# Two pair blocks at the end of each expert stage, held on the chip, in a diffusion backbone on one Trainium2 core

## The chip, the core and the metric

The kernel runs as one program on one core of a Trainium2 chip. A core has a matrix engine (TensorE, PE in the profile; PEld is its loading of weights), a vector engine (VectorE, DVE), an engine for activations (ScalarE, ACT), a general engine (GpSimd, POOL), an engine that mostly issues DMAs (SyncE, SP), and 16 DMA engines. TensorE's results go to PSUM banks; everything else lives in on-chip SBUF. The metric is the time of one execution in microseconds on the device; the kernel before took 2634.41 us, the median of three runs (2627.93 to 2635.23).

## What is computed

Two layers over 512 latent tokens (and 256 context tokens in the first), each a token mixer and then a hierarchical mixture of experts: every token is sent to 2 of 32 experts, and the two results, weighted, are added to the token's row. The part that matters here:

```python
    out = lax.map(expert_block, (buf.reshape(n_blocks, MOE_BLOCK, d), block_expert)).reshape(cap, d)
    # expert_block: (silu(xb @ w_gate[e]) * (xb @ w_up[e])) @ w_down[e]
    y = jnp.zeros((n_assign, d), h.dtype).at[order].set(out[dest]).reshape(n_tok, TOP_K, d)
    return jnp.einsum('tk,tkd->td', weights, y)
...
        x = x + gt2 * hier_moe(...)       # d = 1024, hidden width 512, 32 experts, top 2
    return rmsnorm(x, final_g)
```

## The kernel before, in words

Class `Moe` (from line 324) does one expert stage; `m[0]` is layer 0 with n = 6 tiles of 128 tokens, `m[1]` layer 1 with n = 4. After routing, the 32 experts are ranked by their number of tokens. The `big` first ranks (8 in layer 0, 6 in layer 1) get a block of 128 rows each; the others share a block by twos, 64 rows each. So a stage has 20 units (12 pairs and 8 big ones) or 19 (13 and 6). `self.seq` (line 337) is their order: the pair of two experts that are fixed beforehand first, then big ones and pairs mixed evenly; in both layers it ends on a big one and a pair.

A unit's weights come in pieces of 1 MB (`load`, line 486): 6 for a big one, 12 for a pair, in the order gate, up, down. They go through a ring of slots (`slot`, line 451; 13 slots in layer 0, 15 in layer 1), all issued by SyncE in order (line 497). The unit's token rows are gathered from `hbuf` by GpSimd (line 811).

`experts` (line 842) is the loop over units: gate and up products into `gu_ps` (line 901), `hidden` (silu and product, lines 964 and 965), `transposed` (line 855: TensorE transposes into banks of tag `eT`, three of them, then a copy by ScalarE for `hT` or an add by VectorE for `xT`), the down products into `o_ps` (line 918), and `yo` (line 921: VectorE scales by the token's weight and the gate). `scatter` (line 824) writes yo's rows to `ybuf` in DRAM, two rows for each token (GpSimd, indirect DMA).

The last unit is not scattered. Its yo is split into two fp32r parts (`y_parts`, lines 66 and 67) and brought to token order by a product with a matrix of zeros and ones (`one_hot`, line 950), line 942. All other results come back from `ybuf` by `early` (line 869): one load for each tile of 128 tokens (line 874), 1 MB, into slots of the weight ring, issued behind the scatter of the next-to-last unit; GpSimd then adds the two rows of each token (line 877). The end of the stage (lines 933 to 947) goes tile by tile: for two tiles of three VectorE adds the reloaded row sum to x (line 937), for the third TensorE adds it by a product with the identity (line 944); VectorE adds the product to x (line 945); then `after.tile` takes the sum of squares (line 2113) and `after.group` the reciprocal root for a group of tiles (lines 78 to 90). In layer 0 (`Rms`) x goes to DRAM and the RWKV layer follows; in layer 1 (`FinalNorm`) line 2144 makes the results and line 2145 stores them. `overflow` (line 968) is a loop for blocks over 128 rows, which runs zero times if there are none; all engines pass its test.

The order of instructions on each engine is made by the framework's scheduler from the order of the program and its own model, except in `route`, where it is as written. `behind` and `late_table` (lines 737 and 792) are small tables for the overflow, made beside the units 6 and 7, and also use banks of tag `eT`.

Of the kernel before, what the change touches and what calls it, by code (L numbers as in the profile page):

```python
# [9 lines left out]
F32 = mybir.dt.float32  # L10
# [7 lines left out]
P = 128  # L18
# [305 lines left out]
class Moe:  # L324


    def __init__(self, k, l, n):
        self.k, self.l, self.n = k, l, n


        self.big = BIGS[l]
        self.pairs = (NE - self.big) // 2
        self.units = self.big + self.pairs

        self.nb = self.units + (2 * n * P) // 65
        rest, small = range(self.big), range(self.big, self.units - 1)
        self.seq = [self.units - 1] + [u for _, u in sorted(
            [((i + 0.5) / len(rest), u) for i, u in enumerate(rest)] + [((i + 0.6) / len(small), u) for i, u in enumerate(small)])]
        self.raw, self.slots = {}, 0
        self.scattered = []  # L340

# [13 lines left out]
    def open(self, ps, tag):  # L355
# [13 lines left out]
        self.tok = new([n], "tok")  # L369
# [146 lines left out]
    def route(self, rp, ps, after):  # L516
# [165 lines left out]
        u = self.seq[-1]  # L682
# [109 lines left out]
    def late_table(self, ep, ps, place, blocks, a, b, part):  # L792

        k, n, m = self.k, self.n, part.stop - part.start

        def hot(i, t):
            v = ep.tile([P, P], F32R, name="hot", bufs=2)
            k.nc.vector.tensor_scalar(v, k.iota, place[:, i, t:t + 1], None, op0=ALU.is_equal)
            return v

        def rows(i, shape):
            v = ep.tile([P, 512], F32R, name="h_e", bufs=2)[:, 0:n * m * (b - a)]
            return v.rearrange("p (n v b) -> p n v b", n=n, v=m)

        q = ps.tile([P, 4, b - a], F32, name="tab", tag="eT", bufs=3)
        self.table(k.nc.vector, q, rows, hot, blocks, a, b, part)

    def gather(self, b, idx=None):
# [33 lines left out]
    def experts(self, ep, ps, after):  # L842
# [12 lines left out]
        def transposed(src, nj, name, bufs, pin=False):  # L855
            T = ep.tile([P, nj, P], F32, name=name, bufs=bufs)
            for hf in range(nj // 4):
                q = ps.tile([P, 4, P], F32, name="eT_ps", tag="eT", bufs=3)
                for j in range(4):
                    turn = nc.tensor.transpose(q[:, j, :], self.block(src, 4 * hf + j) if nj == KD else src[:, j * P:(j + 1) * P], k.ident)  # L860
                    if pin and j + hf == 0:
                        k.tc.keep_in_program_order(turn)
                if nj == KD:
                    self.shifted(T, q, hf)
                else:
                    nc.scalar.copy(T, q)  # L866
            return T

        def early():

            ys = []
            for t in range(n):
                y = self.slot().rearrange("p (k d) -> p k d", k=2)
                nc.sync.dma_start(y, self.ybuf[2 * t * P:2 * (t + 1) * P, :].rearrange("(p k) d -> p k d", k=2))
                ys.append(y)
# [9 lines left out]
        for i in range(N + 1):  # L885
# [5 lines left out]
            if i < N:  # L891
                want(i + 1)
                if i + XG - 1 < N:
                    xg[i + XG - 1] = self.gather(seq[i + XG - 1])
                q = {}
                for gu in range(2):
                    q[gu] = ps.tile([P, 512], F32, name="gu_ps", tag="gu", bufs=2)
                    for kk in range(KD):
                        f = slice(kk % 4 * 512, kk % 4 * 512 + 512)
                        for r, rows in self.ranks(seq[i]):  # L900
                            mm(q[gu][rows], xT[i][:, kk, rows], self.raw[r, 2 * gu + kk // 4][:, f], start=kk == 0, stop=kk == KD - 1)  # L901
                    if i + gu == 0:
                        xT[1] = transposed(xg[1], KD, "xT", 2, True)
                h = self.hidden(ep, q)
            if i + 2 < N:
                xT[i + 2] = transposed(xg[i + 2], KD, "xT", 2)
            if i == N - 2:
                one_hot = self.one_hot(ep)
            if i >= 1:
                u = seq[i - 1]  # L910
                g = self.gate(ep, self.ctx[:, u:u + 1])
                yo = ep.tile([P, D], F32, name="yo", bufs=YO)
                o = [ps.tile([P, 512], F32, name="o_ps", tag="eo", bufs=2) for _ in range(2)]
                for c in range(4):
                    for hf in range(2):
                        f = slice(c % 2 * 1024 + hf * 512, c % 2 * 1024 + hf * 512 + 512)
                        for r, rows in self.ranks(u):
                            mm(o[hf][rows], hT[i - 1][:, c, rows], self.raw[r, 4 + c // 2][:, f], start=c == 0, stop=c == 3)  # L918
                for hf in range(2):
                    f = slice(hf * 512, hf * 512 + 512)  # L920
                    stt(yo[:, f], o[hf], self.wslot[:, u:u + 1], g[:, f], op0=ALU.mult, op1=ALU.mult)  # L921
                if i < N:
                    self.scatter(u, yo)
                    if i == N - 1:
                        ys = early()
                else:
                    yh, yl = (ep.tile([P, D], F32R, name="y_parts", tag="xT", bufs=2) for _ in range(2))
                    for hf in range(2):
                        f = slice(hf * 512, hf * 512 + 512)
                        split(k, yh[:, f], yl[:, f], yo[:, f])  # L930
            if i < N:
                hT[i] = transposed(h, 4, "hT", 2)
        for g in after.groups:
            for t in g:
                by_pe = t % 3 == 2
                if not by_pe:
                    k.tc.keep_in_program_order(tt(k.x[:, t, :], k.x[:, t, :], ys[t][:, 0, :], op=ALU.add))
                for hf in range(2):
                    f = slice(hf * 512, hf * 512 + 512)
                    q = ps.tile([P, 512], F32, name="c_ps", tag=("gu", "eo")[t % 2], bufs=2)  # L940
                    for j, y in enumerate((yh, yl)):
                        mm(q, one_hot[:, t * P:(t + 1) * P], y[:, f], start=(j == 0), stop=(j == 1 and not by_pe))
# [7 lines left out]
    def one_hot(self, ep):  # L950

        k = self.k
        oh = self.xgp.tile([P, D], F32R, name="xg", bufs=XG)
        for t in range(self.n):
            k.tc.keep_in_program_order(k.nc.vector.tensor_scalar(
                oh[:, t * P:(t + 1) * P], k.iota, self.tok[:, t:t + 1], None, op0=ALU.is_equal))
        return oh

    def hidden(self, ep, q):
# [8 lines left out]
    def overflow(self, ep, ps, after):  # L968
# [5 lines left out]
        with tc.For_i(0, nv) as i:  # L974
# [14 lines left out]
            xg = self.gather(None, idx)  # L989
            xT = self.xgp.tile([P, D], F32, name="xg", bufs=XG).rearrange("p (k s) -> p k s", k=KD)  # L990
            for hf in range(2):
                q = ps.tile([P, 4, P], F32, name="eT_ps", tag="eT", bufs=3)
# [13 lines left out]
            qh = ps.tile([P, 4, P], F32, name="eT_ps", tag="eT", bufs=3)  # L1006
# [32 lines left out]
BIGS, KNOWN = (8, 6), 2  # L1039

RAW = (2, 8, 3), (4, 6, 5)
XG, YO = 4, 3


C = 64
# [1053 lines left out]

class Rms:  # L2100

    groups = ((0, 1), (2, 3), (4, 5))

    def __init__(self, k):
        self.k = k
# [148 lines left out]
```

## Time and profile before

| | us |
|---|---|
| median of the runs (lowest, highest) | 2634.41 (2627.93, 2635.23) |
| the profiled execution | 2646.03 |
| its span, first to last instruction | 2644.2 |
| TensorE busy | 2374.9 (90%) |
| VectorE busy | 1096.4 (41%) |
| ScalarE busy | 723.5 (27%) |
| GpSimd busy | 374.3 (14%) |
| HBM read and written | 580.65 MB and 76.02 MB |

The profiled execution took 11.6 us more than the median. The profile divides its span in 40 equal slices of 66.1 us and gives the busy share of each engine in tenths, the clock that TensorE was granted (1.00 is 2.4 GHz, 0.50 is 1.2 GHz, means lie between), and the DMA engines' mean share and rate. In a timeline a row is one instruction or several alike in sequence (x4): start, time from the first's start to the last's end, engine, line, operation, what it writes and reads. A value in brackets is the engine's idle time just before, and what ended it. TensorE's fp32 products are recorded as two matmuls each, fp32r products as one.

### The profile page before, as it was taken

The numbers are of one execution on the slowest core, as the hardware profiler recorded it, in microseconds if no ns is written. First come the engines' busy times: TensorE is split into PE (matmuls) and PEld (weight loads), VectorE is DVE, ScalarE is ACT, GpSimd is POOL, SyncE is SP. The second block draws the span as 40 slices with busy tenths as digits, with TensorE's granted clock in tenths as the row PEclk, the third lists the DMA queues.
The fourth block names the chain that finished last, engine by engine and source line by source line (L and its number), as shares of the span: only waits on it lengthen the run. The fifth ranks groups of instructions, "written<-read, shape, count | busy, mean of one in ns | idle before, by whom it ended". The sixth has DMA issues, their size and how long they took to land. (4 is left out here: it accounts for less than half of the span.)

```text
span 2644.2 us, 38930 instructions
## 1 busy us (share of the span) xinstructions
PE 2374.9 (90%) x15546; PEld 1503.5 (57%) x15546; DVE 1096.4 (41%) x2016; ACT 723.5 (27%) x1225; POOL 374.3 (14%) x316
## 2 busy tenths in 40 slices
PE   5999999997999999968979899888888799999984
PEld 2878997774434334336745488777877543333331
DVE  3334333443122111178655364887787412211114
ACT  3222213331000000036644246556544200000001
POOL 0000000003332322230012112112212110000001
PEclk8999999997999999979978698989999899999997
DMA  7135316558999999943165464434335699999993
GB/s 249 57 128 187 116 65 212 198 214 345 398 421 393 421 413 421 398 149 100 57 192 160 139 180 122 102 89 98 85 94 167 234 418 420 421 416 413 420 416 158
DMA packets 280077, 640.24 MB, mean 242 GB/s; under 512 B 131084, under 2 KB 156940, under 8 KB 229460
## 3 DMA queue, kind: packets, MB, share of 16 engines
q1 hardware_dynamic: 266548, 608.69, 62.6%
q0 software_dynamic: 11904, 23.77, 2.4%
q10 hardware_dynamic: 1440, 5.24, 0.5%
q8 instruction: 124, 2.03, 0.3%
q14 instruction: 61, 0.50, 0.1%
HBM read 580.65 MB, written 76.02 MB: 248 GB/s over the span
## 5 line engine op out<-in xcount | busy, mean ns | idle before, releaser
L901 PE MATMUL gu_ps<-e_raw,xT 128*64 128x512 f32 (+1 forms) x2048 | 582.7, 596 | 15.7 <-DMA e_raw<-moe_w_up 13.5
L901 PEld LDWEIGHTS gu_ps<-e_raw,xT 128*64 128x64 f32 (+1 forms) x2048 | 210.0, 148 | 371.1 <-issue 324.0
L918 PE MATMUL o_ps<-e_raw,hT 128*64 128x512 f32 (+1 forms) x1024 | 295.9, 603 | 5.0 <-ACT hT L866 5.0
L965 DVE TENSOR_TENSOR h_e<-gu_ps,h_e 128x512 f32<-128x512 f32 x39 | 27.0, 692 | 483.2 <-PE gu_ps L901 483.2
L918 PEld LDWEIGHTS o_ps<-e_raw,hT 128*64 128x64 f32 (+1 forms) x1024 | 105.7, 149 | 157.2 <-issue 142.9
L964 ACT ACTIVATE h_e<-gu_ps 128x512 f32<-128x512 f32 x39 | 23.3, 597 | 568.3 <-PE gu_ps L901 568.3
L1134 PE MATMUL p<-ident 128*128 128x128 f32 x892 | 138.4, 298 | 8.8 <-ACT BKt L1819 4.7
L1134 PEld LDWEIGHTS p<-ident 128*128 128x128 f32 x892 | 116.6, 201 | 21.2 <-ACT BKt L1819 6.5
L866 ACT COPY hT<-eT_ps 128x512 f32<-128x512 f32 x39 | 22.9, 586 | 349.4 <-PE eT_ps L860 349.4
L825 POOL DMA_INDIRECT ybuf<-yo,idx x37 | 37.0, 1000 | 456.3 <-DVE yo L921 401.2
L921 DVE SCALAR_TENSOR_TENSOR yo<-o_ps,wslot,gt_e 128x512 f32<-128x512 f32 x40 | 30.0, 751 | 170.6 <-issue 120.7
L811 POOL DMA_INDIRECT xg<-hbuf,idx x39 | 41.4, 1061 | 397.3 <-PE eT_ps L860 322.3
L73 PE MATMUL u_ps<-hh,w_hi 128*128 128x384 f32 x256 | 90.2, 353 | 4.8 <-ACT w_hi L66 4.8
L921 DVE SCALAR_TENSOR_TENSOR yo<-o_ps,wslot,gt2B 128x512 f32<-128x512 f32 x38 | 28.5, 751 | 153.0 <-PE o_ps L918 151.3
L75 PE MATMUL u_ps<-hh,w_lo 128*128 128x384 f32 x256 | 86.0, 340 | 1.2 <-DVE w_lo L67 1.2
L74 PE MATMUL u_ps<-hl,w_hi 128*128 128x384 f32 x256 | 87.0, 340 | 0.0
L67 DVE TENSOR_TENSOR w_lo<-w_raw,w_hi 128x1024 fp32r<-128x1024 f32 x56 | 68.1, 1222 | 40.4 <-ACT w_hi L66 39.7
L123 PE MATMUL ada_ps<-w_raw,cstat 128*32 128x512 f32 x384 | 63.8, 633 | 20.6 <-DMA w_raw<-ada_w 20.3
L73 PE MATMUL v_ps<-w_hi,hh 128*128 128x512 f32 x192 | 75.5, 406 | 4.2 <-ACT w_hi L66 4.2
L1849 DVE TENSOR_TENSOR X<-X,subt 128x31 f32<-128x31 f32 (+15 forms) x186 | 75.2, 404 | 5.2 <-DVE subt L1844 0.2
L66 ACT CAST w_hi<-w_raw 128x1024 fp32r<-128x1024 f32 x56 | 58.5, 1048 | 64.4 <-DMA w_raw<-ga_w_out 28.4
L75 PE MATMUL v_ps<-w_hi,hl 128*128 128x512 f32 x192 | 75.7, 394 | 0.0
(561 smaller groups left out, 4444.9 us busy)
## 6 DMA issues: line engine op xcount, KB each, us to landing
e_raw<-moe_w_gate SPq DMA_DIRECT2D x128, 1024.0 KB
e_raw<-moe_w_up SPq DMA_DIRECT2D x128, 1024.0 KB
e_raw<-moe_w_down SPq DMA_DIRECT2D x128, 1024.0 KB
w_raw<-ada_w SPq DMA_DIRECT2D x96, 512.0 KB
w_raw<-ga_w_in SPq DMA_DIRECT2D x32, 512.0 KB
Td<-c_st SPq DMA_DIRECT2D x64, 192.0 KB
T<-Td SPq DMA_DIRECT2D x24, 512.0 KB
ybuf<-zero_rows SPq DMA_DIRECT2D x20, 512.0 KB
```

Source lines behind the costliest of these rows:

```text
L66: k.nc.scalar.copy(hi, src)
L67: k.nc.vector.tensor_tensor(lo, src, hi.bitcast(F32), op=ALU.subtract)
L73: mm(out, a[0], b[0], start=start, stop=False)
L74: mm(out, a[0], b[1], start=False, stop=False)
L75: mm(out, a[1], b[0], start=False, stop=stop)
L123: nc.tensor.matmul(q[32 * g:32 * g + 32, :], k.cstat[:, j, :], w, start=(j < 4), stop=(j >= 4), tile_position=(0, 32 * g))
L811: k.nc.gpsimd.indirect_dma_start(out=xg[:], out_offset=None, in_=self.hbuf[:, :], in_offset=bass.IndirectOffsetOnAxis(ap=self.idx[:, 1, b: ...
L901: mm(q[gu][rows], xT[i][:, kk, rows], self.raw[r, 2 * gu + kk // 4][:, f], start=kk == 0, stop=kk == KD - 1)
L918: mm(o[hf][rows], hT[i - 1][:, c, rows], self.raw[r, 4 + c // 2][:, f], start=c == 0, stop=c == 3)
L921: stt(yo[:, f], o[hf], self.wslot[:, u:u + 1], g[:, f], op0=ALU.mult, op1=ALU.mult)
L1134: nc.tensor.matmul(q[:, 0:128], self.ident, self.ident, start=True, stop=True)
L1849: eng.tensor_tensor(x, x, t.t.rearrange("p (a b) -> p a b", a=31 - j), op=ALU.subtract)
```

## The change

- `HELD = 2`: the last two units of `seq` are pairs, taken from the end of the ranks; the others are mixed as before. In layer 0 the order was P PBPBPBPPBPBPBPPBPBP and becomes P BPPBPBPBPBPBPBPBPPP; in layer 1 it was P PBPPBPPBPPBPPBPPBP and becomes P PBPBPPBPPBPBPPBPPP (P a pair, B a big one).
- Neither of the two is scattered. The down products of the next-to-last unit come ahead of the last unit's gate and up; its two parts take buffers of the ring `yo`, and its products into token order (`add`) are placed one step (tile and half) at a time between the last unit's gate and up products, in banks of tag `c` and `eT` alternately, each followed by VectorE's add to x.
- `early` is called ahead of that, behind the last weights. GpSimd adds no rows. At the end, for even tiles VectorE adds both reloaded rows to x; for odd tiles TensorE adds both by identity products in the bank of the last unit's rows.
- Tag `eT` has two banks in place of three, the third goes to `c`. `tok` is made by one broadcast add for each held unit. A square root of one column is put behind the last silu. Layer 0's groups become (0, 1, 2, 3) and (4, 5).

```diff
+        small, last = small[:len(small) - HELD], list(small[len(small) - HELD:])
         self.seq = [self.units - 1] + [u for _, u in sorted(
-            [((i + 0.5) / len(rest), u) ...] + [((i + 0.6) / len(small), u) for i, u in enumerate(small)])]
+            [((i + 0.5) / len(rest), u) ...] + [((i + 0.6) / len(small), u) for i, u in enumerate(small)])] + last
...
-        for t in range(n):
-            ts(self.tok[:, t:t + 1], tab[0][:, 1, u:u + 1], float(BIG - t * P), None, op0=ALU.add)
+        for i, u in enumerate(self.seq[-HELD:]):
+            tt(self.tok[:, i, :], tab[0][:, 1, u:u + 1].to_broadcast([P, n]), self.off, op=ALU.add)
...
-                q = ps.tile([P, 4, P], F32, name="eT_ps", tag="eT", bufs=3)
+                q = ps.tile([P, 4, P], F32, name="eT_ps", tag="eT", bufs=2)
...
             for t in range(n):
-                y = self.slot().rearrange("p (k d) -> p k d", k=2)
-                nc.sync.dma_start(y, self.ybuf[2 * t * P:2 * (t + 1) * P, :]...)
-            for y in ys:
-                nc.gpsimd.tensor_tensor(y[:, 0, :], y[:, 0, :], y[:, 1, :], op=ALU.add)
+                ys.append(self.slot().rearrange("p (k d) -> p k d", k=2))
+                nc.sync.dma_start(ys[t], self.ybuf[2 * t * P:2 * (t + 1) * P, :]...)
...
+        def output(i):
...
+            parts = None
+            if i >= N - HELD:
+                tag, bufs = ("yo", YO) if i < N - 1 else ("xT", 2)
+                parts = [ep.tile([P, D], F32R, name="y_parts", tag=tag, bufs=bufs) for _ in range(2)]
...
+            if not parts:
+                self.scatter(u, yo)
+            return parts
+
+        def add(one_hot, parts, t, hf, tag, more=()):
+            q = ps.tile([P, 512], F32, name="c_ps", tag=tag, bufs=2 if tag != "c" else 1)
+            for j, y in enumerate(parts):
+                mm(q, one_hot[:, t * P:(t + 1) * P], y[:, half(hf)], start=(j == 0), stop=(j == 1 and not more))
+            for j, y in enumerate(more):
+                mm(q, k.ident, y[:, half(hf)], start=False, stop=(j + 1 == len(more)))
+            tt(k.x[:, t, half(hf)], k.x[:, t, half(hf)], q, op=ALU.add)
...
+            if i == N - 1:
+                ys = early()
+                hot = self.one_hot(0)
+                parts = output(i - 1)
+                steps = [(t, hf) for t in range(n) for hf in range(2)]
...
+                    if steps and gu * KD + kk > 2:
+                        t, hf = steps.pop(0)
+                        add(hot, parts, t, hf, ("c", "eT")[hf])
...
+            if 1 <= i < N - 1:
+                output(i - 1)
+            if i == N - 1:
+                hot = self.one_hot(1)
+                nc.scalar.activation(self.sm.tile([P, 1], F32, name="root"), k.ones[:, 0:1], AF.Sqrt)
+            hT[i] = transposed(h, 4, "hT", 2)
+        parts = output(N - 1)
+        junk = self.xgp.tile([P, D], F32, name="xg", bufs=XG)
         for g in after.groups:
             for t in g:
-                by_pe = t % 3 == 2
-                if not by_pe:
-                    k.tc.keep_in_program_order(tt(k.x[:, t, :], k.x[:, t, :], ys[t][:, 0, :], op=ALU.add))
+                if t % 2 == 0:
+                    for y in range(2):
+                        tt(k.x[:, t, :], k.x[:, t, :], ys[t][:, y, :], op=ALU.add)
                 for hf in range(2):
...
-                    if by_pe:
-                        nc.tensor.matmul(q, k.ident, ys[t][:, 0, f], start=False, stop=True)
-                    tt(k.x[:, t, f], k.x[:, t, f], q, op=ALU.add)
-                after.tile(t, ys[t][:, 1, :])
+                    add(hot, parts, t, hf, ("gu", "eo")[t % 2], [ys[t][:, y, :] for y in range(2)] if t % 2 else ())
+                after.tile(t, junk)
...
-    groups = ((0, 1), (2, 3), (4, 5))
+    groups = ((0, 1, 2, 3), (4, 5))
```

## Rows read from the trace of the kernel before

**Rows 1.** The page: DMA share of 40 slices in tenths.

```profile
DMA  7135316558999999943165464434335699999993
```

**Rows 2.** Windows: busy time of each engine, granted clock, DMA share, GB/s.

```profile
core 0: us, PE busy (x) PEld busy (x) DVE busy (x) ACT busy (x) POOL busy (x), PEclk, DMA share, GB/s
...
760.00:780.00 20.00, 16.46 (x68) 6.82 (x64) 10.20 (x35) 0.59 (x1) 3.48 (x2) 0.83 1.01 419
...
2560.00:2580.00 20.00, 18.42 (x47) 7.37 (x45) 2.22 (x6) 1.18 (x2) 0.00 (x0) 1.00 1.01 419
...
2580.00:2590.00 10.00, 10.00 (x49) 3.43 (x50) 0.75 (x1) 0.60 (x1) 0.97 (x1) 1.00 0.62 257
...
2610.00:2620.00 10.00, 6.52 (x14) 3.35 (x12) 7.24 (x9) 3.78 (x6) 1.40 (x1) 0.59 0.00 0
```

**Rows 3.** Timeline of PE, two waits for weights: start, us, what, idle before.

```profile
650.85 3.65 PE L901 MATMUL gu_ps<-e_raw,xT 128*64 128x512 f32 x16 [1.68 <-DMA e_raw<-moe_w_up]
...
2541.93 3.65 PE L901 MATMUL gu_ps<-e_raw,xT 128*64 128x512 f32 x14 [1.30 <-DMA e_raw<-moe_w_up]
```

**Rows 4.** Timeline of SP: issues of weights and of the reload.

```profile
1094.92 7.75 SPq L497 DMA_DIRECT2D e_raw<-moe_w_down  x4
...
2512.80 9.07 SPq L497 DMA_DIRECT2D e_raw<-moe_w_up  x4
...
2569.94 7.77 SPq L497 DMA_DIRECT2D e_raw<-moe_w_down  x4
2589.37 1.86 SPq L874 DMA_DIRECT2D e_raw<-ybuf  x4
```

**Rows 5.** Timeline of PE: the last unit's down products in either layer.

```profile
1122.09 7.14 PE L918 MATMUL o_ps<-e_raw,hT 128*64 128x512 f32 x32 [0.73 <-ACT hT L866]
...
2596.15 7.14 PE L918 MATMUL o_ps<-e_raw,hT 128*64 128x512 f32 x32 [0.73 <-ACT hT L866]
```

**Rows 6.** Timeline of POOL: its adds of reloaded rows in either layer.

```profile
1126.26 16.84 POOL L877 TENSOR_TENSOR e_raw<-e_raw 128x1024 f32<-128x1024 f32 x6 [18.19 <-DMA e_raw<-ybuf]
...
2601.13 10.27 POOL L877 TENSOR_TENSOR e_raw<-e_raw 128x1024 f32<-128x1024 f32 x4 [19.06 <-DMA e_raw<-ybuf]
```

**Rows 7.** Timeline of DVE (last row ACT): layer 0's last operation, layer 1's end.

```profile
1160.87 0.16 DVE L90 TENSOR_TENSOR rstd<-r34s,r34t 128x2 f32<-128x2 f32 x1
...
2602.47 1.61 DVE L921 SCALAR_TENSOR_TENSOR yo<-o_ps,wslot,gt2B 128x512 f32<-128x512 f32 x2 [7.76 <-PE o_ps L918]
2604.00 5.19 DVE L67 TENSOR_TENSOR y_parts<-yo,y_parts 128x512 fp32r<-128x512 f32 x2
2609.11 3.37 DVE L937 TENSOR_TENSOR x_res<-x_res,e_raw 128x1024 f32<-128x1024 f32 x1
...
2613.79 1.22 DVE L937 TENSOR_TENSOR x_res<-x_res,e_raw 128x1024 f32<-128x1024 f32 x1
2615.04 1.28 DVE L945 TENSOR_TENSOR x_res<-x_res,c_ps 128x512 f32<-128x512 f32 x2
...
2631.57 1.28 DVE L2144 SCALAR_TENSOR_TENSOR yo<-x_res,rstd,fgB 128x1024 f32<-128x1024 f32 x1
...
2629.00 1.06 ACT L2113 ACTIVATE e_raw<-x_res 128x1024 f32<-128x1024 f32 x1 [4.83 <-DMA out_dram<-yo]
```

**Rows 8.** Timeline of PE: fp32r products, transposes, identity products, a big unit.

```profile
250.40 0.34 PE L73 MATMUL u_ps<-hh,w_hi 128*128 128x384 f32 x1
250.57 0.34 PE L74 MATMUL u_ps<-hl,w_hi 128*128 128x384 f32 x1
...
923.44 1.49 PE L860 MATMUL eT_ps<-ident,xg 128*128 128x128 f32 x8
...
1143.52 3.60 PE L944 MATMUL c_ps<-e_raw,ident 128*128 128x512 f32 x4
...
2555.46 14.00 PE L901 MATMUL gu_ps<-e_raw,xT 128*128 128x512 f32 x32
```

**Rows 9.** The instructions of line 684: ns shortest/median/longest.

```profile
L684 DVE TENSOR_SCALAR tok<-tab x10: 134/136/136, 611.2 to 2100.7; 128x1 f32<-128x1 f32 x10
```

More of the change, by code (lines that the diff above doesn't have):

```diff
@@ L336, in __init__ @@
         rest, small = range(self.big), range(self.big, self.units - 1)
+        small, last = small[:len(small) - HELD], list(small[len(small) - HELD:])
         self.seq = [self.units - 1] + [u for _, u in sorted(
-            [((i + 0.5) / len(rest), u) for i, u in enumerate(rest)] + [((i + 0.6) / len(small), u) for i, u in enumerate(small)])]
+            [((i + 0.5) / len(rest), u) for i, u in enumerate(rest)] + [((i + 0.6) / len(small), u) for i, u in enumerate(small)])] + last
         self.raw, self.slots = {}, 0
@@ L368, in open @@
         self.wslot, self.ctx = new([self.nb], "wslot"), new([self.nb], "ctx")
-        self.tok = new([n], "tok")
+        self.tok, self.off = new([HELD, n], "tok"), new([n], "tok_off")
+        ts(self.off, k.iota[:, 0:n], -float(P), float(BIG), op0=ALU.mult, op1=ALU.add)
         self.oh = new([2, n, 32], "oh")
@@ L803, in rows @@
             return v.rearrange("p (n v b) -> p n v b", n=n, v=m)
-        q = ps.tile([P, 4, b - a], F32, name="tab", tag="eT", bufs=3)
+        q = ps.tile([P, 4, b - a], F32, name="tab", tag="eT", bufs=2)
         self.table(k.nc.vector, q, rows, hot, blocks, a, b, part)
@@ L872, in early, with half @@
             for t in range(n):
-                y = self.slot().rearrange("p (k d) -> p k d", k=2)
-                nc.sync.dma_start(y, self.ybuf[2 * t * P:2 * (t + 1) * P, :].rearrange("(p k) d -> p k d", k=2))
-                ys.append(y)
-            for y in ys:
-                nc.gpsimd.tensor_tensor(y[:, 0, :], y[:, 0, :], y[:, 1, :], op=ALU.add)
-            return ys
+                ys.append(self.slot().rearrange("p (k d) -> p k d", k=2))
+                nc.sync.dma_start(ys[t], self.ybuf[2 * t * P:2 * (t + 1) * P, :].rearrange("(p k) d -> p k d", k=2))
+            return ys
+        def half(hf):
+            return slice(hf * 512, hf * 512 + 512)
+        def output(i):
+            u = seq[i]
+            g = self.gate(ep, self.ctx[:, u:u + 1])
+            yo = ep.tile([P, D], F32, name="yo", bufs=YO)
+            o = [ps.tile([P, 512], F32, name="o_ps", tag="eo", bufs=2) for _ in range(2)]
+            for c in range(4):
+                for hf in range(2):
+                    f = slice(c % 2 * 1024 + hf * 512, c % 2 * 1024 + hf * 512 + 512)
+                    for r, rows in self.ranks(u):
+                        mm(o[hf][rows], hT[i][:, c, rows], self.raw[r, 4 + c // 2][:, f], start=c == 0, stop=c == 3)
+            parts = None
+            if i >= N - HELD:
+                tag, bufs = ("yo", YO) if i < N - 1 else ("xT", 2)
+                parts = [ep.tile([P, D], F32R, name="y_parts", tag=tag, bufs=bufs) for _ in range(2)]
+            for hf in range(2):
+                stt(yo[:, half(hf)], o[hf], self.wslot[:, u:u + 1], g[:, half(hf)], op0=ALU.mult, op1=ALU.mult)
+                if parts:
+                    split(k, parts[0][:, half(hf)], parts[1][:, half(hf)], yo[:, half(hf)])
+            if not parts:
[8 more added lines that the diff above has]
+            tt(k.x[:, t, half(hf)], k.x[:, t, half(hf)], q, op=ALU.add)
         xg, xT, hT = {}, {}, {}
@@ L884, in experts @@
         xT[0] = transposed(xg[0], KD, "xT", 2)
-        for i in range(N + 1):
+        for i in range(N):
             if i == BEHIND:
@@ L890, in experts @@
                     self.late_table(ep, ps, self.place_ov, self.block_ov, self.units, self.nb, part)
[L891 to L904, printed above, removed]
+            want(i + 1)
@@ new lines, in experts @@
+            if i + XG - 1 < N:
+                xg[i + XG - 1] = self.gather(seq[i + XG - 1])
+            steps = []
+            if i == N - 1:
[3 more added lines that the diff above has]
+                steps = [(t, hf) for t in range(n) for hf in range(2)]
+            q = {}
+            for gu in range(2):
+                q[gu] = ps.tile([P, 512], F32, name="gu_ps", tag="gu", bufs=2)
+                for kk in range(KD):
+                    f = slice(kk % 4 * 512, kk % 4 * 512 + 512)
+                    for r, rows in self.ranks(seq[i]):
+                        mm(q[gu][rows], xT[i][:, kk, rows], self.raw[r, 2 * gu + kk // 4][:, f], start=kk == 0, stop=kk == KD - 1)
+                    if steps and gu * KD + kk > 2:
+                        t, hf = steps.pop(0)
+                        add(hot, parts, t, hf, ("c", "eT")[hf])
+                if i + gu == 0:
+                    xT[1] = transposed(xg[1], KD, "xT", 2, True)
@@ L905, in experts @@
+            h = self.hidden(ep, q)
             if i + 2 < N:
                 xT[i + 2] = transposed(xg[i + 2], KD, "xT", 2)
[L907 to L930, printed above, removed]
@@ L938, in experts @@
                 for hf in range(2):
[L939 to L942, printed above, removed]
-                    if by_pe:
-                        nc.tensor.matmul(q, k.ident, ys[t][:, 0, f], start=False, stop=True)
-                    tt(k.x[:, t, f], k.x[:, t, f], q, op=ALU.add)
@@ L955, in one_hot @@
             k.tc.keep_in_program_order(k.nc.vector.tensor_scalar(
[L956 removed]
+                oh[:, t * P:(t + 1) * P], k.iota, self.tok[:, i, t:t + 1], None, op0=ALU.is_equal))
         return oh
@@ L991, in overflow @@
             for hf in range(2):
-                q = ps.tile([P, 4, P], F32, name="eT_ps", tag="eT", bufs=3)
+                q = ps.tile([P, 4, P], F32, name="eT_ps", tag="eT", bufs=2)
                 for j in range(4):
@@ L1005, in overflow @@
             hT = ep.tile([P, 4, P], F32, name="hTo", tag="h_e", bufs=2)
-            qh = ps.tile([P, 4, P], F32, name="eT_ps", tag="eT", bufs=3)
+            qh = ps.tile([P, 4, P], F32, name="eT_ps", tag="eT", bufs=2)
             for j in range(4):
@@ L1041 @@
 RAW = (2, 8, 3), (4, 6, 5)
-XG, YO = 4, 3
+XG, YO, HELD = 4, 3, 2
 C = 64
```

5 lines of the change are left out of this document (1 added, 4 removed).

## The prediction

> **What bounds the kernel now.** I read the page's slices first: DMA engines are busy at 9 tenths in the 11th to 17th and the 33rd to 39th slice [rows 1]. Those are the two expert stages, layer 0 until some 1130 us and layer 1 from some 2110 to 2603. Only their ends, and what follows until the next stage, can be touched by this change, so the second view is the windows of the ends and the third the timelines there, engine by engine.
>
> In layer 1 weights arrive without a gap (419 GB/s, share 1.01) until 2580, then the share falls to 0.62 [rows 2]. TensorE is busy 18.4 of 20 us, yet it still waits for weights at 2541.93 [rows 3]. When does the last weight land? SyncE issued the piece awaited there as the last of four at 2512.80 + 9.07 - 0.33 = 2521.5; TensorE went on at 2541.93. So a piece lands 20.4 us after its issue. The last weight was issued at 2569.94 + 7.77 - 0.33 = 2577.4 [rows 4], so it lands near 2597.8, although the share falls at 2580: some DMA engines are done early while others still have a backlog. The last product uses it from its second half on, 2596.15 + 3.57 = 2599.7, and ends at 2603.29 [rows 5]. There TensorE has 1.9 us of slack against DMA. With the same lag layer 0's last weight lands at 1094.92 + 7.75 - 0.33 + 20.4 = 1122.7 against a use at 1122.09 + 3.57 = 1125.7: slack 3.0 us, end 1129.23.
>
> Behind that end stands a chain on VectorE. GpSimd adds the two rows of each token (10.27 us in layer 1, 16.84 in layer 0), because the reload of rows waited for a scatter: issued 2589.37, landed 2601.13 [rows 4, 6]. While GpSimd adds, VectorE's operations are stretched: two halves of y_parts take 5.19 us and the first row add 3.37; the same add later takes 1.22 [rows 7]. From the last product to the last result VectorE's chain is 2632.85 - 2603.29 = 29.6 us in layer 1 and 1161.03 - 1129.23 = 31.8 us in layer 0 [rows 5, 7].
>
> **The change part by part.**
>
> *Order of units, scatter gone.* The weights are the same 192 pieces per layer. One scatter, of the next-to-last unit, falls away: 0.5 MB, at 419 GB/s an estimate of 1.25 us of DMA time ahead of the last weight. Layer 1 ends on pair, pair, pair. Each pair brings 12 MB (30 us at that rate) and costs TensorE 14 us of gate and up, 7.1 of down, 2.2 of turns between, about 23. So at this end TensorE waits for DMA: last weight 2597.8 - 1.25 = 2596.6, then half a product, 3.57, gives 2600.2, with 0.2 for the wake-up 2600.4: **2.9 us earlier**. Layer 0 is different: there TensorE runs without waits (its only long one is 1.68 us at 650.85 [rows 3]), a ring of 13 pieces lets DMA lead by one pair only, and pair, pair, pair at the end uses up that lead without emptying it. So its end goes with TensorE's own work, bounded below by DMA: 1122.7 - 1.25 + 3.57 = 1125.0, that is -4.2 us.
>
> *Held products.* The next-to-last unit's rows are added by fp32r products inside the last unit's gate and up: 6 tiles x 2 halves x 2 parts = 24 in layer 0, 16 in layer 1. One of 384 columns follows the next after 0.17 us [rows 8]; for 512 I estimate 0.23. That is 5.5 us and 3.7 us. In layer 1 they lie in waits for weights: from 2571, when the unit before is done by the same lag, 14 + 3.7 us reach 2588.7, while the last up piece is used until 2590. In layer 0 nothing covers them: +5.5 on the path. VectorE's 12 (8) adds of 0.64 (two in 1.28 [rows 7]) run under them; each step waits for the bank that the add two steps before empties (0.46 + 0.64 us against 1.8 us for two steps), and behind a step that waits stand the last unit's gate and up on TensorE, so its whole end.
>
> *Transposes with two banks in place of three.* hT takes one bank, xT two; xT's second half must now wait for the copy of hT. Eight transposes take 1.49 us [rows 8], so the second half begins 0.75 us behind hT's last one, by when ScalarE has had as long for its copy of hT: next to nothing in steady state. During the late tables, which hold a bank, TensorE already idles 3.5 us in 20 [rows 2]; bounds 0 and +5 a layer (that idle time once more and half again); I take +0.5, nearest to the steady state, in layer 0 and none in layer 1, where a wait for weights follows. The first waits of layer 0 (unit 1 becomes a big one): -2.0 to 0, I take -2.0. So layer 0's last product ends at +5.5 - 2.0 + 0.5 = **+4.0** (bounds -4.2 to +10).
>
> *Reload.* It is issued behind the weights without the scatter's wait. On the engines that are late it follows the weights at once as before, so in layer 1 the four land from 2601.13 - 1.25 = 2599.9 on, 2.5 us apart; the chain wants them at about 2602.5, 2604, 2608 and 2608.5. It costs and wins nothing by itself. Between it and the weights nothing else stands on SyncE; behind it wait only the stores of x, which need the sums anyway. In layer 0 the six rows need 15 us behind the weights, up to 1137 or 1141, and are wanted from 1135 to 1150.
>
> *VectorE's chain, layer 1.* GpSimd's adds are gone, and with them the stretching. From the end of the product: 2.1 us until y_parts are done (two halves at 0.65, about half a row add each, the first 0.8 behind the product with its half of yo and a cast); tile 0 has two row adds of 1.22 and two product adds in 1.28: 5.8; tile 1 two product adds: 7.1; tile 2 with 0.5 for small operations: 11.3; five small operations of 0.2: 12.3; two results of 1.24: 14.8; six small ones 16.0; a result 17.3; tile 3: 18.6; square 1.06 and its read-out 0.2, small ones 1.4, the last result 1.28: 22.5 [rows 7]. TensorE must keep up: an odd tile now has four fp32r and four identity products, the latter two records each of 0.44 (32 such records in 14.00 us [rows 8]): 0.9 + 3.5 = 4.4 us at the high clock, an even one 0.9, so 5.3 us a couple of tiles against VectorE's 5.2. I add 1.5 us for waits: 24.0 against 29.6, **-5.6**.
> *Layer 0* in the same way: 2.1 + 3 x 5.2 + 1.0 (first group's small ones, one group fewer) + 1.3 + 2.9 (last square and its small ones) = 22.9, with 0.8 of wake-ups 23.7, and 2.5 for TensorE: 26.2 against 31.8, **-5.6**. What follows, the loop test and the next stage, shifts with it.
> *Routing:* ten operations of 0.136 [rows 9] become four of like size: -0.7 (bounds -0.8 to 0). The first operand "off", the second one-hot and the early square root lie beside other work: one sits in phase A's end, the others under products; without that cover each costs under 1.3 us.
>
> Sum: layer 0 +4.0 - 5.6 = -1.6; layer 1 -2.9 - 5.6 = -8.5; routing -0.7; together **-10.8**. The profiled execution took 2646.0 (span 2644.2), so it would take 2635.2; the median of the runs is 2634.4, 11.6 lower, and goes to **2623.6**, written 2624. 0.3% is 7.9 us, about what a measurement can tell from no change: below 2626.5 is faster, above 2642.3 slower.
>
> **The rivals.**
> 1. *DMA is really done when its share falls.* For it: 0.62 from 2580 [rows 2], 257 GB/s for 10 us or 2.6 MB, which would end the weights at some 2587. Then in layer 1 the product ends 2587 + 3.8 = 2591, 12 us earlier in place of 2.9, and the sum is -20: 2614. Against it: the lag of 20.4 us, and the first row's landing at 2601.13, 11.8 us behind its issue. The Trainium skill (DMA: Bandwidth & Descriptors, "Why a DMA increments its semaphore by 16 and not by 1") says that a transfer runs on up to 16 engines that finish independently and has landed only with the last of them. By that rule a mean share can't date the last weight and the forecast stands, by the share alone this rival would; no row here shows the engines apart. Chance 0.14.
> 2. *The end side is eaten in layer 0.* Two banks delay turns and late tables, held products wait for their one bank "c": the product ends at +10 in place of +4, and VectorE's order puts a row add in front of yo before its row has landed (+2.5). Sum -2.3: 2632. For it: layer 0 has no cover. Chance 0.24.
> 3. *TensorE at the low clock bounds both tails: slower.* The granted clock is 0.59 in the tail [rows 2], a mix of 2.4 and 1.2 GHz, after TensorE had stood with little work between its last product and y_parts. At 1.2 GHz four identity records take 3.60 us in layer 0's tail [rows 8], 0.88 each with pipelining; an odd tile takes 4 x 0.46 + 8 x 0.88 = 8.9 us, a couple 10.7. Layer 1's tail is then 2.5 + 2 x 10.7 + 4.8 = 28.7 (-0.9), layer 0's 2.5 + 3 x 10.7 + 3.7 = 38.3 (+6.5). Sum: 4.0 + 6.5 - 2.9 - 0.9 - 0.7 = +6.0: 2640, and 2646 with layer 0's product at +10. It is slower than before from 9.5 us a couple on (five couples, 6 us over 5 below 10.7). Against it: TensorE now has work almost all the time from y_parts on. Chance 0.14.
>
> **How the numbers follow.** Forecast 0.48, between -4 and -18 by the bounds; some 0.35 of it lies below 2626.5. With rival 1 faster has 0.49. Rival 3 has half beyond 2642.3, rival 2 and the forecast's tail 0.03 more: slower 0.10. Same: 0.41. The range goes from 2609 (rival 1 with the lower bound of layer 0's end) to 2640 (rival 3), which leaves out about 0.17.
>
> **What would show it.** Right: no GpSimd add; y_parts at 0.7 us a half; layer 1's last product ends 2 to 4 us earlier by the stage's own start, with waits for the last down piece; layer 0's ends up to 10 us later. Wrong: an end 10 us earlier in layer 1 (rival 1), VectorE waiting for c_ps of odd tiles several us each with clock near 0.5 (rival 3), TensorE gaps before transposes (rival 2), or VectorE waiting for a reload ahead of yo.

## The result, and the profile after

The changed kernel takes 2656.0 us (median of 10 runs, 2651.3 to 2664.7) beside 2640.2 (10 runs, 2627.9 to 2644.7) of the kernel before: ratio 1.0061, interval 1.0044 to 1.0078. It is **slower by 0.6%**, where 2624 was predicted and 2640 was the upper end of the range. The profiled execution took 2656.15 us (span 2654.4) beside 2646.03 (span 2644.2). Stage by stage, in us of the two profiled executions:

| stretch | before | after | change | predicted |
|---|---|---|---|---|
| layer 0, first gate product to end of last down product | 505.0 | 532.3 | +27.3 | +4.0 |
| layer 0, from there to the last rstd | 31.8 | 21.3 | -10.5 | -5.6 |
| between the layers (nothing changed there) | 951.8 | 947.2 | -4.7 | -0.7 |
| layer 1, first gate product to end of last down product | 490.4 | 497.0 | +6.6 | -2.9 |
| layer 1, from there to the last result | 29.6 | 20.2 | -9.4 | -5.6 |

So both tails gained more than forecast, and the weight stages lost it all and more. First the windows that are exactly the two stages; columns as in [rows 2]. Of the changed kernel:

```profile
core 0: us, PE busy (x) PEld busy (x) DVE busy (x) ACT busy (x) POOL busy (x), PEclk, DMA share, GB/s
624.70:1156.99 532.29, 496.36 (x1816) 197.94 (x1816) 98.89 (x193) 26.18 (x43) 141.72 (x76) 0.99 0.96 391
2125.43:2622.42 496.99, 468.03 (x1789) 186.56 (x1788) 81.93 (x168) 25.03 (x42) 32.14 (x32) 0.99 0.99 407
```

Of the kernel before:

```profile
624.18:1129.22 505.04, 482.99 (x1793) 195.47 (x1792) 87.28 (x173) 24.95 (x41) 145.22 (x78) 0.99 0.99 410
2112.87:2603.29 490.42, 460.17 (x1773) 182.12 (x1772) 74.47 (x154) 23.80 (x40) 35.13 (x34) 1.00 1.00 412
```

In layer 0 TensorE is idle 35.9 us in place of 22.1 (+13.9) and busy 13.4 longer, while the DMA share falls from 0.99 to 0.96: DMA now waits for the ring that TensorE empties. SyncE's issues of weights there waited 275 us in all for products of TensorE to free a slot, 110 us in the kernel before. What is TensorE idle for? The waits of PE over the whole execution (us in total, times, longest), of the changed kernel:

```profile
PE eT_ps L861 <- DVE xT L823: 47.3, 29, 4.3
...
PE gu_ps L939 <- DMA e_raw<-moe_w_up: 3.6, 3, 2.3
PE eT_ps L861 <- DVE h_e L983: 3.4, 4, 0.9
```

and of the kernel before:

```profile
PE eT_ps L860 <- DVE h_e L965: 31.0, 33, 3.5
...
PE gu_ps L901 <- DMA e_raw<-moe_w_up: 13.5, 11, 1.7
```

The transposes of h_e waited 31.0 us in 33 units for h_e itself. Now they wait 47.3 us in 29 units for another operation, an add into xT, which h_e doesn't need. One unit of the changed kernel, PE and then DVE (start, us, what, idle before):

```profile
986.26 0.63 PE L861 MATMUL eT_ps<-ident,h_e 128*128 128x128 f32 x4 [1.54 <-DVE xT L823]
986.81 1.55 PE L861 MATMUL eT_ps<-ident,xg 128*128 128x128 f32 x8
988.30 7.14 PE L891 MATMUL o_ps<-e_raw,hT 128*64 128x512 f32 x32
...
984.82 0.69 DVE L983 TENSOR_TENSOR h_e<-gu_ps,h_e 128x512 f32<-128x512 f32 x1 [9.76 <-PE gu_ps L939]
985.43 1.28 DVE L823 TENSOR_TENSOR xT<-eT_ps,shift 128x512 f32<-128x512 f32 x2
```

and the same place of the kernel before, PE from the unit before on and then DVE:

```profile
973.91 1.49 PE L860 MATMUL eT_ps<-ident,xg 128*128 128x128 f32 x8
...
998.55 0.66 PE L860 MATMUL eT_ps<-ident,h_e 128*128 128x128 f32 x4 [0.85 <-DVE h_e L965]
999.19 1.49 PE L860 MATMUL eT_ps<-ident,xg 128*128 128x128 f32 x8
...
998.41 1.28 DVE L822 TENSOR_TENSOR xT<-eT_ps,shift 128x512 f32<-128x512 f32 x2
```

Read the order on VectorE: h_e first, then the two xT adds. The transposes that those adds empty ran behind the unit before, and ended 23 us earlier in the kernel before (975.40 against 998.41) and 24 us earlier in the changed one: they sit in their two banks through all of gate and up, because the xT buffer they go into is the one that these products read. With three banks h_e's transposes took the third and started 0.85 us behind gate and up. With two there is none, so they wait for the first xT add, 0.69 us more, in nearly every unit.

The clock adds to it. Of the changed kernel and then of the kernel before:

```profile
900.00:920.00 20.00, 18.37 (x52) 7.14 (x50) 1.89 (x3) 0.59 (x1) 1.09 (x1) 0.91 0.88 349
1060.00:1080.00 20.00, 18.37 (x53) 6.77 (x53) 3.07 (x5) 0.58 (x1) 0.00 (x0) 0.91 0.53 216
```

```profile
900.00:920.00 20.00, 19.98 (x66) 8.59 (x65) 1.50 (x2) 0.74 (x2) 7.31 (x4) 1.00 1.02 421
1060.00:1080.00 20.00, 18.38 (x83) 6.33 (x83) 2.64 (x4) 1.18 (x2) 6.25 (x3) 1.00 1.02 421
```

0.91 is a mix of 2.4 with some 1.2 GHz; in both windows of the changed kernel it follows a wait of 1.54 us. The DMA share of 0.53 fits a full ring: from 1045 to 1080 us SyncE's issues waited 29.6 us for TensorE's products and for nothing else.

The end of layer 1 on VectorE and TensorE, of the changed kernel, beside [rows 7]:

```profile
2623.13 0.68 DVE L67 TENSOR_TENSOR y_parts<-yo,y_parts 128x512 fp32r<-128x512 f32 x1
2623.72 1.22 DVE L961 TENSOR_TENSOR x_res<-x_res,e_raw 128x1024 f32<-128x1024 f32 x1
2624.86 0.69 DVE L67 TENSOR_TENSOR y_parts<-yo,y_parts 128x512 fp32r<-128x512 f32 x1
...
2641.37 1.28 DVE L2163 SCALAR_TENSOR_TENSOR yo<-x_res,rstd,fgB 128x1024 f32<-128x1024 f32 x1
...
2626.17 3.59 PE L910 MATMUL c_ps<-e_raw,ident 128*128 128x512 f32 x8
```

y_parts takes 0.7 us a half (5.19 for two in [rows 7]), a row add 1.22 (3.37), and eight identity records 3.59, at the high clock, where four took 3.60 in [rows 8].

### The profile page after: what moved, and what is told of

It reads as the page before. It is cut to its first block, busy times and chain, and to the rows that moved or that the text cites. A ratio compares the mean times of both kernels' runs of the same rounds, so it can differ in the third digit from the quotient of the medians.

```text
span 2654.4 us, 39078 instructions
## 1 busy us (share of the span) xinstructions
PE 2397.3 (90%) x15614; PEld 1510.7 (57%) x15614; DVE 1103.3 (42%) x2043; ACT 725.4 (27%) x1230; POOL 345.1 (13%) x304
## 5 line engine op out<-in xcount | busy, mean ns | idle before, releaser
L891 PE MATMUL o_ps<-e_raw,hT 128*64 128x512 f32 (+1 forms) x1024 | 305.0, 611 | 4.8 <-ACT hT L867 4.8
L74 PE MATMUL v_ps<-w_lo,hh 128*128 128x512 f32 x192 | 75.7, 396 | 0.0
L74 PE MATMUL o_ps<-w_lo,gh 128*128 128x512 f32 x192 | 75.7, 396 | 0.0
## 6 DMA issues: line engine op xcount, KB each, us to landing
e_raw<-moe_w_gate SPq DMA_DIRECT2D x128, 1024.0 KB, 20.2
```

The lines of the kernel that those rows point to most:

```text
L74: mm(out, a[0], b[1], start=False, stop=False)
L891: mm(o[hf][rows], hT[i][:, c, rows], self.raw[r, 4 + c // 2][:, f], start=c == 0, stop=c == 3)
```

## The experiments

Each profiled execution is cut as above: a stage runs from its layer's first gate product to the end of its last down product, the tail from there to the last rstd or result. The lengths are in us, and the ratio is to runs of the kernel before on the same chip.

| kernel | layer 0 stage, tail | layer 1 stage, tail | ratio (interval) |
|---|---|---|---|
| before | 505.0, 31.8 | 490.4, 29.6 | |
| changed | 532.3, 21.3 | 497.0, 20.2 | 1.0061 (1.0044 to 1.0078) |
| after_three_banks | 514.9, 21.3 | 489.1, 20.2 | 0.9965 (0.9942 to 0.9988) |
| before_two_banks | 519.6, 29.8 | 490.8, 29.3 | 1.0059 (1.0023 to 1.0094) |
| before_new_order | 509.3, 31.7 | 490.2, 30.8 | 1.0008 (0.9987 to 1.0029) |
| before_new_tail | 504.7, 21.2 | 490.5, 20.2 | 0.9936 (0.9912 to 0.9961) |
| before_two_banks_three_xT | 504.2, 31.7 | 490.4, 29.6 | 1.0021 (1.0002 to 1.0040) |
| three_banks_old_order | 512.7, 21.3 | 496.3, 20.2 | 0.9969 (0.9953 to 0.9986) |
| changed_split_turns | 505.6, 21.3 | 491.6, 20.2 | 0.9940 (0.9921 to 0.9960) |
| new_tail_split_turns | 504.7, 21.2 | 493.2, 20.2 | 0.9948 (0.9923 to 0.9972) |
| new_tail_idle_adds | 504.7, 28.4 | 490.3, 29.0 | 0.9980 (0.9963 to 0.9996) |
| held_in_layer_1_only | 504.4, 21.3 | 489.6, 20.2 | 0.9928 (0.9901 to 0.9954) |

**A third bank for the changed kernel.**

```diff
-                q = ps.tile([P, 4, P], F32, name="eT_ps", tag="eT", bufs=2)
+                q = ps.tile([P, 4, P], F32, name="eT_ps", tag="eT", bufs=3)
...
```

> The changed kernel with a third PSUM bank for the transposes; all else as changed. Theory A (bank): in the changed kernel the transposes of h_e wait 1.54 us a unit for VectorE's first xT add, 0.85 us for h_e alone in the kernel before; with three banks the wait is 0.85 again, and TensorE's gaps of over 1 us are gone, the granted clock in layer 0 with them back at 0.99 from 0.96. Layer 0's last down product then ends near 1141 to 1146 (changed: 1156.99), layer 1 is bound by DMA again, and the kernel takes 2625 to 2637 us. Theory B (order of units: three pairs at the end, a big one second): no more than 4 us better, 2650 to 2656. Theory C (held products and what they bring): 2646 to 2652, since only waits in cover of DMA come back.

2629.7 us, 26 below the changed kernel's median; layer 0's last product ends at 1137.3, earlier than expected. The wait on xT is gone from the list of waits:

```profile
PE eT_ps L861 <- DVE h_e L983: 31.0, 33, 3.6
...
PE gu_ps L939 <- DMA e_raw<-moe_w_up: 9.1, 8, 2.1
```

and the granted clock of the two windows above is 1.00. (Over layer 0's whole stage it is 0.99 with and without the third bank; the 0.96 in the expectation is the DMA share.) Theory A holds: the bank costs 17.4 us in layer 0 and 7.9 in layer 1. It was there to be had: with two, gate and up use two banks, down two, the held block one, the transposes two, and the eighth was unused. The Trainium skill (Perfetto Trace Analysis, "Matmul Optimizations") asks to make sure that all 8 PSUM banks are used; these two kernels agree, 26 us for the eighth, but changed_split_turns below is no slower with seven.

**Two banks for the kernel before**, the same edit backwards.

> The kernel before with two PSUM banks for the transposes in place of three; all else as before. Theory A: h_e's transposes wait 1.54 us in place of 0.85 in about 15 units of either layer, layer 0's last product ends 10 to 17 us later than 1129.23, layer 1 (which has 13.7 us of waits for weights) loses 3 to 8 us: 2650 to 2664. Theories B and C: as before, 2634 to 2644.

2654.8 us, theory A. The wait appears in the untouched program, and over the whole execution it sums to the same 47.3 us in 29 times. In layer 0 alone:

```profile
PE eT_ps L860 <- DVE xT L822: 25.8, 15, 4.2
```

against 17.3 in 17 times for h_e before. Layer 1 loses 0.4 us only, less than the 3 to 8 expected: it has 21.5 us of waits for xT, but its waits for weights fall from 13.7 us to 2.8.

**The order of units alone.**

```diff
+        small, last = small[:len(small) - 2], list(small[len(small) - 2:])
         self.seq = [self.units - 1] + [u for _, u in sorted(
...
+            [...]) ] + last
```

> The kernel before with the new order of units alone (a big unit second, three pairs last); three banks, the next-to-last unit is scattered, GpSimd adds the rows. Theory B: layer 0's last product ends 8 us or more later, 2648 or more. Theory A: within 4 us of the kernel before, 2636 to 2644, with the first waits of layer 0 changed by 2 us at most.

2640.2 us, no measurable change, as A has it; but layer 0's stage is 4.3 us longer. Its waits for weights are 5.6 us in place of 2.0; until 760 us they are 3.8 in place of 1.7, about what A allowed for the first waits, and the rest comes later.

**The tail alone.**

```diff
-            for y in ys:
-                nc.gpsimd.tensor_tensor(y[:, 0, :], y[:, 0, :], y[:, 1, :], op=ALU.add)
...
-                by_pe = t % 3 == 2
+                by_pe = t % 2 == 1
                 if not by_pe:
-                    k.tc.keep_in_program_order(tt(k.x[:, t, :], k.x[:, t, :], ys[t][:, 0, :], op=ALU.add))
+                    for y in range(2):
+                        tt(k.x[:, t, :], k.x[:, t, :], ys[t][:, y, :], op=ALU.add)
...
-    groups = ((0, 1), (2, 3), (4, 5))
+    groups = ((0, 1, 2, 3), (4, 5))
```

> The kernel before with the tail's additions alone: no GpSimd add, both rows of a token added by VectorE (even tiles) or by identity products (odd tiles), two groups in layer 0; the next-to-last unit is still scattered and the reload waits for it. In the changed kernel the tails shrank from 31.8 to 21.3 us and from 29.6 to 20.2. Theory A1 (the gain is GpSimd's adds and the stretching of VectorE beside them): both tails shrink by 8 to 10 us here too, 2622 to 2628. Theory A2 (the gain needs the reload without the scatter's wait): rows land from 2601 on and VectorE stands for them, tails shrink by 3 to 5 us, 2630 to 2636.

2622.7 us, 15 below the kernel before: theory A1. Both tails are those of the changed kernel to 0.1 us, though the scatter and the reload's wait for it are still there. All that the change gained comes from this part; holding back a second block adds nothing to it. No kernel tried is measurably faster than this one.

**What GpSimd's adds do to VectorE.** The adds are put back, into a tile that nobody reads.

```diff
+            beside = self.xgp.tile([P, D], F32, name="xg", bufs=XG)
+            for y in ys:
+                nc.gpsimd.tensor_tensor(beside, y[:, 0, :], y[:, 1, :], op=ALU.add)
```

> The kernel before with the new tail, and GpSimd's adds of the two rows put back with a result that nobody reads: nothing waits for them, and only what GpSimd's work does to VectorE beside it is left of the old tail. Tails with the new additions: 21.2 and 20.2 us; the old ones 31.8 and 29.6. Theory S (VectorE's operations are stretched while GpSimd adds: two halves of y_parts 5.19 us in the kernel before, 1.4 without): the tails grow back by 3 to 8 us each, 2627 to 2637. Theory T (the old tail was long because its sums came late, behind the adds): both tails stay within 1 us of 21.2 and 20.2, 2620 to 2625.

2639.0 us, 2 above the range of theory S, and the tails are 28.4 and 29.0: theory S in the tails, 7.2 and 8.8 us for work that nothing waits for. Its end of layer 1, POOL, then DVE:

```profile
2595.65 10.86 POOL L878 TENSOR_TENSOR xg<-e_raw 128x1024 f32<-128x1024 f32 x4 [18.88 <-DMA e_raw<-ybuf]
...
2597.18 1.61 DVE L922 SCALAR_TENSOR_TENSOR yo<-o_ps,wslot,gt2B 128x512 f32<-128x512 f32 x2 [7.76 <-PE o_ps L919]
2598.70 2.30 DVE L67 TENSOR_TENSOR y_parts<-yo,y_parts 128x512 fp32r<-128x512 f32 x1
2600.92 3.39 DVE L940 TENSOR_TENSOR x_res<-x_res,e_raw 128x1024 f32<-128x1024 f32 x1
2604.23 2.82 DVE L67 TENSOR_TENSOR y_parts<-yo,y_parts 128x512 fp32r<-128x512 f32 x1
2606.98 1.21 DVE L940 TENSOR_TENSOR x_res<-x_res,e_raw 128x1024 f32<-128x1024 f32 x1
...
2611.78 0.69 DVE L949 TENSOR_TENSOR x_res<-x_res,c_ps 128x512 f32<-128x512 f32 x1 [2.20 <-PE c_ps L948]
```

Until GpSimd ends at 2606.5, operations that read two SBUF tiles (y_parts, x_res) take 2.8 to 4 times as long. yo, with one operand in PSUM, takes 1.61 us for its two halves with GpSimd beside it and without. The Trainium skill (SBUF — State Buffer, "SBUF: two separate sides") says that a VectorE instruction with two SBUF inputs and a GpSimd one that reads SBUF exclude each other for a whole instruction; the trace agrees, with 2.82 against 0.68 us. In layer 0 this lengthening is the whole 7.2 us. In layer 1 it is 5.9 of the 8.8; most of the rest comes by way of TensorE, which stands 4.87 us for a lengthened half of y_parts. Its granted clock from 2605 to 2610 us is 0.50 (1.2 GHz), six identity records take 5.10 us, and VectorE waits 3.0 us for products (2.20 of them in the last row) in place of 0.3.

**Why two banks are too few.**

```diff
-                xT[i + 2] = transposed(xg[i + 2], KD, "xT", 2)
+                xT[i + 2] = transposed(xg[i + 2], KD, "xT", 3)
...
-XG, YO = 4, 3
+XG, YO = 4, 2
```

> The kernel before with two PSUM banks for the transposes, but three xT buffers in SBUF in place of two (yo has two buffers in place of three to make room). Theory A, its mechanism: TensorE runs xT's transposes a unit ahead; VectorE can't empty their banks into xT until gate and up of the unit have read the old xT out of that buffer, so both banks stay full until the unit's end and h_e finds no third. With a third xT buffer the banks are emptied in the middle of a unit, h_e's transposes wait 0.85 us again and not 1.54, and layer 0's last product ends near 1130 (kernel before 1129.22, with two banks alone 1144.49): 2634 to 2644 us. Rival: two banks are too few whatever the buffers are, since three tiles of transposes belong to each unit: as with two banks alone, 2650 to 2660.

2644.7 us, 0.7 above the range of theory A, and layer 0's stage 504.2 in place of 519.6: theory A's mechanism. The ratio is still 1.0021, and the stages and tails don't show where that lies. A unit of it:

```profile
999.77 0.66 PE L860 MATMUL eT_ps<-ident,h_e 128*128 128x128 f32 x4 [0.85 <-DVE h_e L965]
1000.26 0.65 PE L860 MATMUL eT_ps<-ident,xg 128*128 128x128 f32 x4
1001.15 0.75 PE L860 MATMUL eT_ps<-ident,xg 128*128 128x128 f32 x4 [0.25 <-ACT hT L866]
...
1000.94 0.69 DVE L822 TENSOR_TENSOR xT<-eT_ps,shift 128x512 f32<-128x512 f32 x1 [1.23 <-PE eT_ps L860]
```

The adds now follow the transposes at once, into a free buffer. What is left is a wait of 0.25 us for the copy of hT.

**The other way to empty the banks early:** the changed kernel with its two banks, but half of xT's transposes ahead of h_e's and half behind, pinned behind gate and up of the same unit.

```diff
             for hf in range(nj // 4):
+                if hf and between:
+                    between()
                 q = ps.tile([P, 4, P], F32, name="eT_ps", tag="eT", bufs=2)
...
-                xT[i + 2] = transposed(xg[i + 2], KD, "xT", 2)
+                def turn_h(i=i, h=h):
+                    hT[i] = transposed(h, 4, "hT", 2, True)
+                xT[i + 2] = transposed(xg[i + 2], KD, "xT", 2, True, turn_h)
```

> The changed kernel, two banks kept, with another order of the transposes on TensorE: first half of the next xT behind gate and up of the unit, then h_e's, then xT's second half, in place of h_e's first and xT's run a unit ahead. Theory A, its mechanism: banks are now emptied within some 1.5 us of being filled, so two banks are enough, and the first half covers the wait for h_e: waits ahead of h_e's transposes below 0.4 us in place of 1.54, layer 0's last product 17 to 28 us earlier than 1156.99, 2615 to 2632 us. Rival: two banks are too few; the second half waits for the first half's add, 0.7 us a unit stay, 2640 to 2656.

2623.3 us, 33 below the changed kernel, with the same two banks: theory A. The wait ahead of h_e's transposes in the steady state is 0.39 us, and layer 0's stage is 505.6:

```profile
991.05 0.66 PE L863 MATMUL eT_ps<-ident,h_e 128*128 128x128 f32 x4 [0.39 <-DVE h_e L988]
```

**The same order on top of the new tail**, three banks.

> The kernel before with the new tail alone (2622.7 us) and the same order of transposes, three banks. Theory A and what it leaves open: in layer 0 TensorE still waits 0.85 us a unit for h_e; with half of xT's transposes in that place layer 0's stage shrinks by 17 x 0.7 = 12 us, to some 493 us, unless DMA bounds it first (0.9 to 1.0 of its time is used); layer 1, bound by DMA, keeps its 490. So 2608 to 2616. Rival: layer 0 is bound by DMA as well as soon as TensorE gains, 2618 to 2623.

2624.7 us: the rival in kind, 1.7 above its range. The waits of PE in layer 0:

```profile
PE eT_ps L862 <- DVE h_e L970: 8.6, 17, 2.9
PE o_ps L920 <- ACT hT L868: 4.9, 16, 0.7
PE gu_ps L901 <- DMA e_raw<-moe_w_up: 4.8, 4, 1.5
PE gu_ps L901 <- DMA e_raw<-moe_w_gate: 3.6, 4, 1.6
```

The waits for h_e halve (17.3 us without the new order of transposes), those for hT grow from 2.5 to 4.9 and those for weights from 2.8 to 8.4, and the stage keeps its 504.7 us with a DMA share of 1.00. So DMA bounds layer 0 as well, at some 504 us. That the kernel before stood on this floor too is read from its share of 0.99; no run lightened DMA alone.

**The held block without the new order**, three banks (the changed kernel with the order of before).

> The changed kernel with three banks and with the order of units of the kernel before, so that what is left of the change is the held block with its products and the new tail. The kernel before with the new tail alone took 2622.7 us, the changed kernel with three banks 2629.7. Theory P (the 24 products that nothing covers in layer 0 cost 5.5 us, and the order cost the rest, some 4 us in layer 0): layer 0's stage of 505 us becomes 510.5, 2625 to 2629. Theory Q (the held block costs nothing, the order all): layer 0's stage 505, 2619 to 2624. Theory R (the held block costs all): stage 514, 2628 to 2633.

2631.7 us, stage 512.7, between P and R and nearer to R (in this order the held unit is a big one): the held block costs 8.0 us in layer 0 over the new tail alone, the new order 2.2 more. TensorE is busy 490.08 us there against 481.76 without the held block: 8.3 us for 24 products, 0.35 each. In layer 1 it costs 5.8 here, and nothing with pairs at the end (489.1).

**Holding in layer 1 only.**

> The changed kernel with three banks, but in layer 0 the order of units of before, no held block and the scatter back; layer 1 as changed. If the sums of the stages add up, layer 0's stage takes 505 us (DMA bounds it as well), layer 1's 489 to 490, the tails 21 and 20: 2619 to 2624, not to be told from the new tail alone (2622.7). Rival: the held block's products cost layer 1 some 6 us, as with the old order of units (496.3): 2626 to 2630.

2625.3 us, between the two ranges; the stages tell them apart: the sums add up (504.4 and 489.6), and the 0.9 us that holding saves in layer 1 can't be measured.

## Why the prediction was wrong, step by step

- **What bounds it now**: half wrong. For layer 1, that weights bound it and TensorE has little slack stands. For layer 0 it was read that "TensorE runs without waits" and DMA leads; it runs without waits for weights, but its 17.3 us of waits for h_e bring it to the same 505 us as DMA's floor (new_tail_split_turns). Where two bounds lie together, help for one of them alone gains nothing, and what hurts one counts.
- **Transposes with two banks**, the step that failed: "next to nothing in steady state", +0.5, bounds 0 to +5 a layer. The runs show +17.4 and +7.9. The step let xT's second half wait for the copy of hT. That is what happens with three xT buffers (0.25 us a unit), not here: it asked when a bank is filled, and not when VectorE may empty it. The rows for that were in the trace of before: the xT adds of a unit stand behind h_e and not behind their transposes, which end 23 us earlier. Of the 17.4 us, 10 are the longer waits (27.5 for xT and h_e against 17.3) and 6 TensorE's longer busy time (496.4 against 490.5). TensorE works 13.7 us of this stage at 1.2 GHz and 5.3 with three banks, so by my estimate (half of the difference) the clock makes some 4 of these 6. Layer 0's stage adds up: 504.7 with the new tail alone, 8.0 for the held block, 2.2 for the order and 17.4 for the bank make the 532.3 measured.
- **Rival 2** named this place (two banks delay the turns) with 0.24, but priced it by the same bounds, at +10 for all of layer 0.
- **The range**: its lower end, 2609, doesn't follow from its two terms (rival 1's 2614 with -4.2 in place of +4.0 in layer 0 is 2606). The result missed the range at its other end.
- **Order of units**: first waits "-2.0 to 0" became +2.1, all waits for weights +3.6 and the stage +4.3 in layer 0 with the order alone (+2.2 beside the held block); the sign was wrong. Layer 1's end, predicted 2.9 us earlier, is 1.3 earlier with three banks; in the changed kernel TensorE is the bound there and nothing of it is seen.
- **Held products**: 24 times 0.23 = 5.5 us in layer 0; measured 8.0 alone (5.6 where the new order is there already). The cost on the path is right in kind and too small. Eight of them take 2.61 us in the changed kernel. They start 0.23 us apart, as estimated; but TensorE runs four steps in a row and not one at a time, and waits in between for the adds of VectorE that empty their banks, which had been taken as covered.

```profile
1126.78 2.61 PE L908 MATMUL c_ps<-y_parts,xg 128*128 128x512 f32 x8
```

- **The tails**: right in mechanism, twice as large as sized. 21.3 and 20.2 us in place of 26.2 and 24.0. The 2.5 and 1.5 us added for TensorE and waits were not needed, and the last tile's adds ran ahead of the third result. GpSimd's adds alone, with what follows from them, make 7.2 and 8.8 us, where 5.6 had been allowed for the whole edit.
- **Reload**: right, it wins and costs nothing; the tail with the scatter's wait is as long.
- **Routing**, -0.7: nothing. The tok operations lie in VectorE's wait for the exponential (1.34 us before, 1.46 after).
- **Rival 3** (low clock in the tails): did not come. Eight identity records take 3.59 us; the clock is 0.98 in layer 0's tail and 0.88 in layer 1's. In layer 1's tail of new_tail_idle_adds something of the kind is seen: 0.50 behind the wait for y_parts.
- **Rival 1** (weights done when the share falls): speaks of an end 12 us earlier, which no run shows, not even with three banks.

What stays open: why the granted clock falls behind some waits of 1.54 us and not behind all. No run changed the clock alone.

## What to carry to other kernels

Before a ring of banks is cut, look up for each tile when its reader may run, not only how long it runs: a reader that writes into a buffer still in use holds the bank until that buffer is free. Where two engines bound a stage within a per cent, price every edit as a loss only, and try its parts one by one: here one part of four held all of the gain. Adds that GpSimd makes beside a VectorE chain can cost that chain more than they take off it.

## What the runs showed that was not expected

The stretch between the layers, which no kernel here changes, took 939.2 us in one profile and 952.7 in another with the same 8842 or 8843 TensorE records. The first is before_new_order, the second held_in_layer_1_only:

```profile
1167.09:2106.27 939.18, 834.40 (x8842) 663.53 (x8843) 631.18 (x1175) 482.75 (x859) 157.11 (x173) 0.89 0.46 131
```

```profile
1149.56:2102.22 952.66, 848.17 (x8843) 673.40 (x8843) 631.94 (x1175) 482.79 (x860) 156.15 (x174) 0.88 0.46 128
```

TensorE's busy time differs by 13.8 us. The low clock falls on other products: TensorE works 159 us of this stretch at 1.2 GHz in the first and 189 in the second. A profiled span can thus move by 13 us with nothing changed, which is more than most edits here; lengths of stages tell more than spans.
